# A state space's injection operator made in the layout of its use, from powers laid out through memory, in a hybrid convolution and S5 layer on one Trainium2 core

## The chip, the core and the metric

The kernel runs on one core of a Trainium2 chip. Its engines take their instructions in order, each from its own queue: TensorE (PE) for matmuls and transposes, VectorE (DVE) and ScalarE (ACT) for elementwise work, GpSimd (POOL), and SyncE (SP), which here issues all DMAs. The metric is the device time of one execution in microseconds (us), as a median over runs. The weights' and inputs' layout in the chip's memory is made on the host before, which isn't timed.

## What is computed

One layer over 1024 positions of 1024 channels. In short, with all else of the reference cut:

```python
h = rms_norm(x, pre_g)
conv_in, z_c, u_s, z_s, g_c, g_s = split(h @ w_in)
ca, cb = split(conv_in, 2)
cu = causal_depthwise_conv(ca * sigmoid(cb))            # 31 taps
conv_out = (silu(layer_norm(cu)) * silu(z_c)) @ w_conv_out
# S5: 32 groups of 16 channels, each drives 64 complex states
bbar = z * b                # z (zr, zi) from lambda and the step, per state
s[t] = a * s[t-1] + bbar @ u[t];   y[t] = Re(c @ s[t]) + d * u[t]
y = gelu(y);  y = y * sigmoid(y @ w_glu + b_glu)
ssm_out = (y * silu(z_s)) @ w_ssm_out
out = (sigmoid(g_c) * conv_out + sigmoid(g_s) * ssm_out) @ w_out
result = x + rms_norm(out, post_g)
```

The S5 part is computed in 128 blocks of 8 positions. Within a group, the injection operator R takes the 8 x 16 inputs (position j in the block, channel h) of a block to its 128 state numbers (64 real, 64 imaginary): an entry is a power of a, which depends on j and the state, times an entry of bbar, which depends on the state and h. A scan over the 128 blocks then gives the states.

## The kernel before

**Products.** Every projection is a product of 1024 positions with 128 output channels, a *unit*, named by its weight: cb and ca (convolution), gc, gs (gates), zc, zs, glu, so, co. To keep float32's precision the weights and the activations are split in two parts: the high parts wh (ACT, `wsplit_h`) and the remainder wl = wr - wh (DVE, `wsplit_l`, L718) of the raw weight wr. Each step k over 128 input channels makes three passes (wh with xh, wh with xl, wl with xh) of two matmuls of 128x512 (`product`, L735, matmuls at L743). A unit has eight steps, a glu or so unit four. Within the unit before, wh is made at the third step and wl at the fifth, and then SP is given the next raw weight's load (`wload`, L700). Two buffers each are there for wr, wh and wl.

**The order.** Units follow a list: cb0 ca0 gc0 cb1 ca1 gc1 to gc7 cb2 ca2 zc0 zc1 cb3 ca3 zc2 zc3, then the glu units, which need the S5's result y, and the rest. Between the k steps other work is put in by a planner that runs while the program is recorded: `Clock` (L640 to L676) holds tasks written as generators, each `yield cost, delay` says how long VectorE is taken and how long the task then rests, and `tick(1.296)` after each k step runs what is due by this model's time. So the order on each engine is fixed in the program, and moves when a task's steps or delays change. The chip keeps each engine's order and waits on semaphores.

**The state space.** The tasks are `s5_params` (L206 to L366, parameters from lambda and the step) and `s5_chain` (L788), which runs `s5_quarter(c)` (L370) for four quarters c of 8 groups. Numbers behind names, as in RT0, are quarters. A quarter does in order:

- DVE: RT = PR * bbar and tmp = sPI * bsw (L397, L399, by `mul`, L387) and their sum (L401): the injection operator with the states on the partitions, 128x1024; PR, PI and sPI are powers, bsw is bbar with its parts swapped.
- PE: eight transposes rp (L404); ACT: the copy R (L406). Now (j, h) lies on the partitions.
- PE: ep = R times U (L416), the inputs of each block taken to the states. U comes through memory (us_scratch, L200).
- DVE: the output operator O (L387, L417); PE: kp (L437, L438), the 8 x 8 blocks within a block, spread into Mt by eight DMAs (L458).
- DVE: an angle ta, tb, tk, rounded and corrected (L446 to L461); ACT: its sines (L463 to L465); DVE: Et, the scan Zs (L476); a swap of halves Zw by two DMAs (L479); then Zw times the sine and Sx (L490).
- PE: yp (L496, L497); ACT: gelu yt (L501); SP: to ys_scratch and back as y32 in another layout (eight DMAs, L507).

After all quarters y is split into yh and yl (L797, L798) for the glu units. DVE also has the convolution's 31 taps (pp and acc, L545), whose input is ext (L517 to L521), and whose starting values ACT makes (L536 to L538).

128x1024 tiles of all these tasks come from one pool of 21 buffers (`T`). PSUM has two buffers "aux" for the state space and two "mm" for the products.

Of the kernel before, what the change touches and what calls it, by code (L numbers as in the profile page):

```python
# [35 lines left out]
def tile_hybrid_block(  # L36
# [16 lines left out]
    bmat: bass.AP,  # L53
    cmat: bass.AP,
    dmat: bass.AP,
    ident_in: bass.AP,
    cst_in: bass.AP,
    iota_in: bass.AP,
# [2 lines left out]
    nc = tc.nc  # L61
    V, A, G, PE = nc.vector, nc.scalar, nc.gpsimd, nc.tensor
# [10 lines left out]
    zc_scr = nc.dram_tensor("zc_scratch", (8, 128, 1024), F32, kind="Internal").ap()  # L73
    us_scr = nc.dram_tensor("us_scratch", (4, 128, 1024), F32, kind="Internal").ap()
    ys_scr = nc.dram_tensor("ys_scratch", (4, 128, 1024), F32, kind="Internal").ap()
    gc_scr = nc.dram_tensor("gc_scratch", (8, 128, 1024), F32, kind="Internal").ap()

    def T(name, dt=F32):
        return tp.tile([128, 1024], dt, tag="T", name=name)

    def PS(name, tag):
        return ps.tile([128, 1024], F32, tag=tag, name=name)
# [4 lines left out]
    ident = const.tile([128, 128], F32, name="ident")  # L87
    cst = const.tile([128, 4], F32, name="cst")
# [8 lines left out]
    iota = const.tile([128, 128], F32, name="iota")  # L97
# [108 lines left out]
    def s5_params(P):  # L206
# [12 lines left out]
        def tt(o, a, b, op):  # L219
            V.tensor_tensor(out=o, in0=a, in1=b, op=op)  # L220
            return o
# [26 lines left out]
        f = st("turnf")  # L248
        s = st("turns")
# [12 lines left out]
        q3 = nt()  # L262
# [31 lines left out]
        PR = const.tile([128, 9, 32], F32, name="PR")  # L294
        PI = const.tile([128, 9, 32], F32, name="PI")
        sPI = const.tile([128, 9, 32], F32, name="sPI")
# [45 lines left out]
        zr = tt(nt(), n1, n2, ALU.add)  # L342
        zr = tt(st("zr"), zr, rden, ALU.mult)
# [4 lines left out]
        sz = st("sz")  # L348
# [4 lines left out]
        bbar, bsw = bb[:, 0], bb[:, 1]  # L353
        tmp = T("bbtmp")
# [8 lines left out]
        tt(tmp, bmt[:, 0], szb, ALU.mult)  # L363
        yield 1.8, 0
        tt(bsw, bsw, tmp, ALU.subtract)
        P.update(PR=PR, PI=PI, sPI=sPI, nPR=nPR, r8=r8, bbar=bbar, bsw=bsw, tauh=tauh, taul=taul)  # L366

    y32 = {}

    def s5_quarter(c, P):  # L370
        g0 = c * 8
# [2 lines left out]
        def v4(t):  # L374
            return t.rearrange("p (g j h) -> p g j h", g=8, j=8)
# [4 lines left out]
        def pw(t, lo):  # L380
            return t[:, lo:lo + 8, gs].rearrange("p j g -> p g j").unsqueeze(3).to_broadcast([128, 8, 8, 16])

        def bc(t):
            return t[:, gs, :].unsqueeze(2).to_broadcast([128, 8, 8, 16])

        def mul(o, x0, x1):
            V.tensor_tensor(out=o, in0=x0, in1=x1, op=ALU.mult)  # L387

        def pe(f, cost):
            for g in range(8):  # L390
                f(g, slice(g * 128, (g + 1) * 128))
            clk.now += cost


        RT = T(f"RT{c}")
        tmp = T(f"tmp{c}")
        mul(v4(RT), pw(P["PR"], 0), bc(P["bbar"]))  # L397
        yield 1.15, 0
        mul(v4(tmp), pw(P["sPI"], 0), bc(P["bsw"]))  # L399
        yield 1.15, 0  # L400
        V.tensor_tensor(out=RT, in0=RT, in1=tmp, op=ALU.add)  # L401
        yield 1.15, 2.5
        rp = PS(f"rp{c}", "aux")
        pe(lambda g, s: PE.transpose(rp[:, s], RT[:, s], ident), 0.9)  # L404
        R = T(f"R{c}")
        A.activation(out=R, in_=rp, func=AF.Copy)  # L406
        U = usU[c]

        O1 = T(f"O1_{c}")
# [71 lines left out]
        if c < 3:  # L481
# [7 lines left out]
        V.memset(v3(Sx)[:, :, 0:1], 0.0)  # L489
        V.tensor_tensor(out=v3(Sx)[:, :, 1:128], in0=v3(Et)[:, :, 0:127], in1=v3(Zw)[:, :, 0:127],  # L490
                        op=ALU.subtract)
        yield 1.2, 4.5
        yp = PS(f"yp{c}", "aux")

# [183 lines left out]
    clk = Clock()  # L678
# [108 lines left out]

    def s5_chain():  # L788
        yield from s5_params(P5)
        for c in range(4):  # L790
            while not P5_ready[0]:
                yield 0.0, 0.5
            yield from s5_quarter(c, P5)
        yield 0.0, 5.0
        for c in range(4):
            yh[c], yl[c] = T(f"yh{c}", F32R), T(f"yl{c}", F32R)
            A.activation(out=yh[c], in_=y32[c], func=AF.Copy)  # L797
            V.tensor_tensor(out=yl[c], in0=y32[c], in1=f32(yh[c]), op=ALU.subtract)  # L798
            yield 1.15, 0
        s5_done[0] = True  # L800
        yield 0.0, 0.0
# [301 lines left out]
    for j in range(2):  # L1103
# [9 lines left out]
WARM = 3  # L1113

_INS = ["x", "xt", "w_us", "w_in", "w_co", "w_glu", "w_so", "w_out", "pre_g", "post_g", "conv_w", "chan",
        "bglu", "lam", "bmat", "cmat", "dmat", "ident", "cst", "iota"]


def _layout(inp):
    import numpy as np  # L1120

    f = np.float32
    d = {}
    d["x"] = inp["x"][0]
    d["xt"] = inp["x"][0].reshape(128, 8, 1024).transpose(2, 1, 0).reshape(8, 128, 1024)
    w = inp["w_in"][0]
    d["w_us"] = w[:, 3072:3456].reshape(4, 2, 128, 384).transpose(0, 2, 1, 3).reshape(4, 128, 768)

    def stat(a):
        k, m = a.shape  # L1130
        return a.reshape(k // 128, 128, m // 128, 128).transpose(2, 1, 0, 3).reshape(m // 128, 128, k)

    wi = stat(w)
    d["w_in"] = wi
    d["w_co"] = stat(inp["w_conv_out"][0])
    d["w_glu"] = stat(inp["w_ssm_glu"][0])
    d["w_so"] = stat(inp["w_ssm_out"][0])
    d["w_out"] = inp["w_out"][0].reshape(8, 128, 1024)
    d["pre_g"] = inp["pre_norm_gain"][0].reshape(8, 128).T
    d["post_g"] = inp["post_norm_gain"][0]  # L1140
    cw = np.concatenate([inp["conv_w"][0][::-1], np.zeros((1, 1024), f)], 0)
    d["conv_w"] = cw.reshape(32, 8, 128).transpose(2, 1, 0)
    col = lambda a: a.reshape(-1, 128).T
    d["chan"] = np.stack([col(inp["conv_b"][0]), col(inp["conv_ln_gain"][0]), col(inp["conv_ln_bias"][0])], 1)
    d["bglu"] = col(inp["b_ssm_glu"][0])
    lr, li = inp["ssm_lambda_re"][0].T, inp["ssm_lambda_im"][0].T
    ldt = np.broadcast_to(inp["ssm_log_dt"][0][None, :], (64, 32))
    d["lam"] = np.stack([np.concatenate([a, a], 0) for a in (ldt, lr, li)], 1)
# [35 lines left out]
```

## Time and profile before

| | |
|---|---|
| median of 3 runs | 827.98 us (827.82 to 828.73) |
| the profiled execution | 828.06 us |
| its span | 826.2 us |
| PE busy | 813.8 us |
| DVE busy | 622.7 us |
| ACT busy | 277.6 us |
| mean granted TensorE clock | 0.997 |

The span runs from the first to the last instruction that the profile shows; 1.86 us of the execution lie around it. Busy time is that of an engine's own instructions; an engine that waits, or only issues DMAs, isn't busy. In a timeline row stand the start, the duration, the engine, the line, the operation with output and input, and in brackets an idle time ahead of it and what ended it. Matmuls overlap, so the time that one takes from the engine is read from start to start.

### The profile page before, as it was taken

The page shows a single profiled execution, that of the slowest core. Times are in us where ns is not written, and L with a number is a line of the kernel's source. Part 1 is how long each engine was busy: PE and PEld are TensorE (multiplying, and loading weights), DVE is VectorE, ACT ScalarE, POOL GpSimd, SP SyncE. Part 2 cuts the span into 40 slices and gives each one's busy share as a digit, 9 for nine tenths or more (in the row PEclk, how much of TensorE's full clock was granted, in tenths as well). Part 3 has the DMA queues.
Part 4 walks back from the last instruction along what each step waited for, and adds up shares of the span by engine and source line. Part 5 has one row for each costly group of instructions (what it writes and reads, how often), then busy time and mean ns, then how long its engine had stood idle before and what let it go on. Part 6 is the DMA issues. An engine that isn't in the chain of part 4 may idle for free.

```text
span 826.2 us, 9707 instructions
## 1 busy us (share of the span) xinstructions
PE 813.8 (98%) x3806; PEld 672.6 (81%) x3806; DVE 622.7 (75%) x902; ACT 277.6 (34%) x300; POOL 25.6 (3%) x27
## 2 busy tenths in 40 slices
PE   9999999999999999999999999999999999999996
PEld 6878888888878887888888888888887888888885
DVE  4699897798998989998999889398496644442242
ACT  5862623535315344323321031222257211131121
POOL 3400000000000000000000000000000000000010
PEclk9999999999999999999999999999999999999998
DMA  9703544463534312111112112122262644425142
GB/s 345 282 35 120 168 102 128 100 195 91 137 109 110 106 52 90 51 52 52 39 38 102 52 52 103 51 90 90 102 199 82 229 153 153 153 76 178 61 171 99
DMA packets 40364, 94.97 MB, mean 115 GB/s; under 512 B 8880, under 2 KB 17712, under 8 KB 40320
## 3 DMA queue, kind: packets, MB, share of 16 engines
q1 hardware_dynamic: 40320, 94.36, 34.2%
q8 instruction: 30, 0.49, 0.2%
q14 instruction: 14, 0.11, 0.0%
HBM read 68.00 MB, written 20.97 MB: 108 GB/s over the span
## 4 chain that ended last, share of the span: by engine, by line
PE 76%; DVE 14%; ACT 3%; DMA 3%; issue 2%; POOL 1%; SPq 1%; DVEq 0%; POOLq 0%; ACTq 0%
PE pgs L743 11%; PE pco L743 11%; PE po L1037 10%; PE pcb L743 9%; PE pca L743 8%; PE pzc L743 7%; PE pzs L743 5%; PE pgc L743 5%; PE pso L743 5%; DVE pp L545 3%; PE pgl L743 2%; DVE acc L545 2%; DMA Zw<-Zs 1%; DVE xt L173 1%; PE ep L416 1%
## 5 line engine op out<-in xcount | busy, mean ns | idle before, releaser
L545 DVE SCALAR_TENSOR_TENSOR pp<-ext,cw,pp 128x512 f32<-128x512 f32 x232 | 165.2, 744 | 5.4 <-ACT pp L536 5.4
L545 DVE SCALAR_TENSOR_TENSOR acc<-ext,hs,acc 128x512 f32<-128x512 f32 x120 | 89.3, 744 | 0.0
L1037 PE MATMUL po<-wox,mgh 128*128 128x512 f32 x192 | 52.3, 389 | 0.0
L521 ACT ACTIVATE ext<-ext 128x1179 f32<-128x1179 f32 x8 | 9.5, 1192 | 101.4 <-DVE ext L520 101.4
L1037 PEld LDWEIGHTS po<-wox,mgh 128*128 128x128 f32 x192 | 36.0, 188 | 7.5
L743 PE MATMUL pcb<-xh,wl_cb 128*128 128x512 f32 x128 | 39.6, 391 | 0.9 <-DVE wl_cb L718 0.9
L743 PE MATMUL pgc<-xh,wh_gc 128*128 128x512 f32 x128 | 40.4, 397 | 0.0
L1009 DVE TENSOR_TENSOR sgr<-pco,sgr 128x1024 f32<-128x1024 f32 x8 | 9.8, 1224 | 40.2 <-PE pco L743 40.2
L743 PE MATMUL pca<-xh,wh_ca 128*128 128x512 f32 x128 | 40.0, 393 | 0.0
L743 PE MATMUL pzc<-xh,wh_zc 128*128 128x512 f32 x128 | 39.8, 392 | 0.0
L743 PE MATMUL pgs<-xh,wh_gs 128*128 128x512 f32 x128 | 39.7, 392 | 0.0
L743 PE MATMUL pca<-xh,wl_ca 128*128 128x512 f32 x128 | 39.5, 390 | 0.1
L743 PE MATMUL pcb<-xh,wh_cb 128*128 128x512 f32 x128 | 39.5, 390 | 0.0
L743 PE MATMUL pgc<-xh,wl_gc 128*128 128x512 f32 x128 | 39.5, 390 | 0.0
L743 PE MATMUL pco<-cuh,wl_co 128*128 128x512 f32 x128 | 39.5, 390 | 0.0
L743 PE MATMUL pgc<-xl,wh_gc 128*128 128x512 f32 x128 | 39.5, 389 | 0.0
L743 PE MATMUL pzc<-xl,wh_zc 128*128 128x512 f32 x128 | 39.5, 389 | 0.0
L743 PE MATMUL pgs<-xl,wh_gs 128*128 128x512 f32 x128 | 39.5, 389 | 0.0
L743 PE MATMUL pco<-cuh,wh_co 128*128 128x512 f32 x128 | 39.4, 389 | 0.0
L743 PE MATMUL pca<-xl,wh_ca 128*128 128x512 f32 x128 | 39.4, 389 | 0.0
L743 PE MATMUL pcb<-xl,wh_cb 128*128 128x512 f32 x128 | 39.4, 389 | 0.0
L743 PE MATMUL pco<-cul,wh_co 128*128 128x512 f32 x128 | 39.4, 389 | 0.0
(273 smaller groups left out, 1760.2 us busy)
## 6 DMA issues: line engine op xcount, KB each, us to landing
xt<-in_xt_dram SPq DMA_DIRECT2D x8, 512.0 KB, 6.2
xin<-in_x_dram SPq DMA_DIRECT2D x8, 512.0 KB, 9.8
wr_cb<-in_w_in_dram SPq DMA_DIRECT2D x8, 512.0 KB, 3.4
wr_ca<-in_w_in_dram SPq DMA_DIRECT2D x8, 512.0 KB, 3.2
wr_gc<-in_w_in_dram SPq DMA_DIRECT2D x8, 512.0 KB, 3.9
gc_scratch<-gct SPq DMA_DIRECT2D x8, 512.0 KB, 3.6
wr_zc<-in_w_in_dram SPq DMA_DIRECT2D x8, 512.0 KB, 3.2
zc_scratch<-zct SPq DMA_DIRECT2D x8, 512.0 KB, 2.6
```

The source lines that it names most:

```text
L173: V.scalar_tensor_tensor(out=xraw[k], in0=xraw[k], scalar=gcol[:, k:k + 1], in1=rbc, op0=ALU.mult, op1=ALU.mult)
L416: pe(lambda g, s: PE.matmul(epp[:, s], lhsT=R[:, s], rhs=U[:, s], start=True, stop=True), 1.8)
L521: A.activation(out=ext[:, :, 0:3, 1:132], in_=ext[:, :, 4:7, 0:131], func=AF.Copy)
L545: V.scalar_tensor_tensor(out=o, in0=src(e, r), scalar=w, in1=o, op0=ALU.mult, op1=ALU.add)
L743: PE.matmul(p[:, js(j)], lhsT=lhs[:, ks], rhs=rhs(k, j), start=st, stop=sp_)
L1009: V.tensor_tensor(out=sgt, in0=p, in1=sgt, op=ALU.mult)
L1037: PE.matmul(p[:, js(j)], lhsT=lhs[k][:, s], rhs=rhs[k][:, js(j)], start=st, stop=sp_)
```

## The change

The injection operator is no longer made with the states on the partitions and transposed. Its entries are regrouped: power times z, which depends on j and the state alone, and the raw input matrix b, which is an input of the kernel. Both are brought into the layout with (j, h) on the partitions by DMAs.

- `s5_params` has six more DVE operations of 128x256, which make the powers times z, real and swapped (qpw).
- `inj_powers`: four transposes of them (qp) on PE, one copy qt of 128x512 on ACT, two DMAs that write qs_scratch in memory.
- `inj_in(c)`, for each quarter: two loads of 512 KB of a new input bt, which the host has laid out and repeated (in..c, in..d), and sixteen loads of 64 KB, each of which reads one row of 4 KB of qs_scratch into sixteen partitions (eight each for in..a and in..b). For quarter 0 it stands in `s5_chain` ahead of the quarters with a rest of 7 model us behind it, for the others ahead of the yield at Sx of the quarter before.
- `s5_quarter`: in..a times in..c, in..b times in..d, and their sum, in place and in the same sizes as the three operations of before. The transposes rp and the copy R are gone.

```diff
@@ s5_params
+        qpw = T("qpw")
+        q3 = [qpw[:, i * 256:(i + 1) * 256].rearrange("p (j g) -> p j g", j=8) for i in range(3)]
+        zrj = zr.unsqueeze(1).to_broadcast([128, 8, 32])
+        szj = sz.unsqueeze(1).to_broadcast([128, 8, 32])
+        yield 0.6, 0
+        tt(q3[0], PR[:, 0:8, :], zrj, ALU.mult)
+        tt(q3[2], sPI[:, 0:8, :], szj, ALU.mult)
+        tt(q3[0], q3[0], q3[2], ALU.subtract)
+        yield 1.0, 0
+        tt(q3[1], PR[:, 0:8, :], szj, ALU.mult)
+        tt(q3[2], sPI[:, 0:8, :], zrj, ALU.mult)
+        tt(q3[1], q3[1], q3[2], ALU.add)
+        P["qpw"] = qpw
+        yield 1.0, 0
...
+    def inj_powers(P):
+        qpw = P.pop("qpw")
+        qp = PS("qp", "aux")
+        for b in range(2):
+            for a in range(2):
+                i = (b * 2 + a) * 128
+                PE.transpose(qp[:, i:i + 128], qpw[:, a * 256 + b * 128:a * 256 + b * 128 + 128], ident)
+        clk.now += 0.45
+        qt = T("qt")
+        A.activation(out=qt[:, 0:512], in_=qp[:, 0:512], func=AF.Copy)
+        for b in range(2):
+            nc.sync.dma_start(out=qs_scr[:, 4 * b:4 * b + 4].rearrange("a j g s -> (j g) a s"),
+                              in_=qt[:, b * 256:(b + 1) * 256].rearrange("p (a s) -> p a s", a=2))
+
+    def inj_in(c):
+        inj[c] = [T(f"in{c}{n}") for n in "abcd"]
+        for r in range(2):
+            nc.sync.dma_start(out=inj[c][2 + r], in_=bt[c, r])
+        for r in range(2):
+            for j in range(8):
+                src = qs_scr[r, j, c * 8:c * 8 + 8].rearrange("g s -> (g s)")
+                nc.sync.dma_start(out=inj[c][r][16 * j:16 * j + 16], in_=src.partition_broadcast(16))
...
@@ s5_quarter
-        RT = T(f"RT{c}")
-        tmp = T(f"tmp{c}")
-        mul(v4(RT), pw(P["PR"], 0), bc(P["bbar"]))
+        R, Rb, B0, B1 = inj.pop(c)
+        mul(R, R, B0)
         yield 1.15, 0
-        mul(v4(tmp), pw(P["sPI"], 0), bc(P["bsw"]))
+        mul(Rb, Rb, B1)
         yield 1.15, 0
-        V.tensor_tensor(out=RT, in0=RT, in1=tmp, op=ALU.add)
-        yield 1.15, 2.5
-        rp = PS(f"rp{c}", "aux")
-        pe(lambda g, s: PE.transpose(rp[:, s], RT[:, s], ident), 0.9)
-        R = T(f"R{c}")
-        A.activation(out=R, in_=rp, func=AF.Copy)
+        V.tensor_tensor(out=R, in0=R, in1=Rb, op=ALU.add)
+        del Rb, B0, B1
+        yield 1.15, 0
...
+        if c < 3:
+            inj_in(c + 1)
         yield 1.2, 4.5
...
@@ s5_chain
         yield from s5_params(P5)
+        while not P5_ready[0]:
+            yield 0.0, 0.5
+        inj_powers(P5)
+        yield 0.0, 0.0
+        inj_in(0)
+        yield 0.0, 7.0
         for c in range(4):
-            while not P5_ready[0]:
-                yield 0.0, 0.5
             yield from s5_quarter(c, P5)
```

The planner's order moves with it. On DVE, in the first quarter, from the last parameter operations on (usT are the four blocks of the input u, scaled; wl_cb1 is the remainder of the weights of unit cb1). Before:

```order
L387 TENSOR_TENSOR RT0_713<-PR_402,bb_677 128x1024
L387 TENSOR_TENSOR tmp0_714<-sPI_404,bb_677 128x1024
L401 TENSOR_TENSOR RT0_713<-RT0_713,tmp0_714 128x1024
L192 TENSOR_TENSOR usT1_463<-usT1_463,rbc_433 128x1024
L516 MEMSET ext0_739 128x2x4x4
L517 TENSOR_TENSOR ext0_739<-pca0_622,sg0_641 128x2x4x128
L520 TENSOR_TENSOR ext0_739<-ext0_739 128x528
L387 TENSOR_TENSOR O1_0_769<-nPR_405,cmt_124 128x1024
L387 TENSOR_TENSOR otmp0_771<-PI_403,cmt_124 128x1024
L718 TENSOR_TENSOR wl_cb1_779<-wr_cb1_590,wh_cb1_750 128x1024
```

After, at the same place:

```order
L222 TENSOR_TENSOR qpw_713<-qpw_713 128x256
L194 TENSOR_TENSOR usT1_463<-usT1_463,rbc_433 128x1024
L556 MEMSET ext0_772 128x2x4x4
L557 TENSOR_TENSOR ext0_772<-pca0_622,sg0_641 128x2x4x128
L560 TENSOR_TENSOR ext0_772<-ext0_772 128x528
L194 TENSOR_TENSOR usT2_465<-usT2_465,rbc_433 128x1024
L758 TENSOR_TENSOR wl_cb1_799<-wr_cb1_590,wh_cb1_783 128x1024
L429 TENSOR_TENSOR in0a_742<-in0a_742,in0c_744 128x1024
L429 TENSOR_TENSOR in0b_743<-in0b_743,in0d_745 128x1024
L442 TENSOR_TENSOR in0a_742<-in0a_742,in0b_743 128x1024
L429 TENSOR_TENSOR O1_0_831<-nPR_405,cmt_124 128x1024
```

The products of the injection operator have moved behind usT2 and wl_cb1, and the output operator behind them; on PE, ep of this quarter moves from the eighth step of gc0 to the fifth of cb1, and kp from cb1's third step to its eighth.

On DVE, from the scan of the first quarter to its Sx (wl_gc1 and wl_gc2 are remainders of weights, Et, Zs, Zw tiles of the quarter, pp and acc taps). Before:

```order
L387 TENSOR_TENSOR Et0_809<-Zs0_957,tb0_863 128x1024
L718 TENSOR_TENSOR wl_gc1_991<-wr_gc1_781,wh_gc1_955 128x1024
L545 SCALAR_TENSOR_TENSOR pp0_832<-ext0_739,cw_82,pp0_832 128x512
L545 SCALAR_TENSOR_TENSOR acc0_831<-ext0_739,hs_83,acc0_831 128x4x128
L545 SCALAR_TENSOR_TENSOR pp0_832<-ext0_739,cw_82,pp0_832 128x512
L387 TENSOR_TENSOR Zw0_966<-Zw0_966,tk0_865 128x1024
L489 MEMSET Sx0_1024 128x8
L490 TENSOR_TENSOR Sx0_1024<-Et0_809,Zw0_966 128x8x127
```

After:

```order
L429 TENSOR_TENSOR Et0_872<-Zs0_1018,tb0_925 128x1024
L556 MEMSET ext1_1053 128x2x4x4
L557 TENSOR_TENSOR ext1_1053<-pca1_950,sg1_967 128x2x4x128
L560 TENSOR_TENSOR ext1_1053<-ext1_1053 128x528
L429 TENSOR_TENSOR Zw0_1027<-Zw0_1027,tk0_927 128x1024
L758 TENSOR_TENSOR wl_gc2_1079<-wr_gc2_887,wh_gc2_1064 128x1024
L527 MEMSET Sx0_1089 128x8
L528 TENSOR_TENSOR Sx0_1089<-Et0_872,Zw0_1027 128x8x127
```

The remainder that follows the Et product now follows the product on Zw, and it is that of gc2; wl_gc1 has moved ahead of the scan.

On ACT, around the gelu of the last quarter (yt3), ahead of the glu units (pp2 and acc2 are starting values of the third convolution block, yh the high parts of y). Before:

```order
L710 ACTIVATE wh_zc2_2232<-wr_zc2_2103 128x1024
L501 ACT_TABLE_LOAD
L501 ACTIVATE yt3_2251<-yp3_2234 128x1024
L536 ACTIVATE pp2_2261<-ext2_1938,cw_82 128x512
L537 ACTIVATE pp2_2261<-ext2_1938,nb1_84,cw_82 128x512
L538 ACTIVATE acc2_2260<-ext2_1938,hs_83 128x4x128
L797 ACTIVATE yh0_2324<-y32_0_1092 128x1024
L797 ACTIVATE yh1_2335<-y32_1_1475 128x1024
L521 ACTIVATE ext3_2345<-ext3_2345 128x3x3x131
L710 ACTIVATE wh_zc3_2356<-wr_zc3_2181 128x1024
L797 ACTIVATE yh2_2358<-y32_2_1879 128x1024
L797 ACTIVATE yh3_2368<-y32_3_2281 128x1024
```

After:

```order
L750 ACTIVATE wh_zc2_2273<-wr_zc2_2110 128x1024
L561 ACTIVATE ext3_2339<-ext3_2339 128x3x3x131
L750 ACTIVATE wh_zc3_2350<-wr_zc3_2215 128x1024
L541 ACT_TABLE_LOAD
L541 ACTIVATE yt3_2391<-yp3_2374 128x1024
L576 ACTIVATE pp2_2404<-ext2_1964,cw_82 128x512
L577 ACTIVATE pp2_2404<-ext2_1964,nb1_84,cw_82 128x512
L578 ACTIVATE acc2_2403<-ext2_1964,hs_83 128x4x128
L841 ACTIVATE yh0_2421<-y32_0_1190 128x1024
L841 ACTIVATE yh1_2431<-y32_1_1596 128x1024
L841 ACTIVATE yh2_2442<-y32_2_1997 128x1024
```

yt3 and what follows it now stand behind ext3 and wh_zc3: on PE, yp of the last quarter has moved from the third step of ca3 to the sixth of zc2, while the glu units stay where they were.

More of the change, by code (lines that the diff above doesn't have):

```diff
@@ L55, in tile_hybrid_block @@
     dmat: bass.AP,
+    bt: bass.AP,
     ident_in: bass.AP,
@@ L75, in tile_hybrid_block @@
     ys_scr = nc.dram_tensor("ys_scratch", (4, 128, 1024), F32, kind="Internal").ap()
+    qs_scr = nc.dram_tensor("qs_scratch", (2, 8, 32, 128), F32, kind="Internal").ap()
     gc_scr = nc.dram_tensor("gc_scratch", (8, 128, 1024), F32, kind="Internal").ap()
@@ L365, in s5_params @@
         tt(bsw, bsw, tmp, ALU.subtract)
+        qpw = T("qpw")
[12 more added lines that the diff above has]
+        yield 1.0, 0
         P.update(PR=PR, PI=PI, sPI=sPI, nPR=nPR, r8=r8, bbar=bbar, bsw=bsw, tauh=tauh, taul=taul)
     y32 = {}
+    inj = {}
+    def inj_powers(P):
[19 more added lines that the diff above has]
+                nc.sync.dma_start(out=inj[c][r][16 * j:16 * j + 16], in_=src.partition_broadcast(16))
     def s5_quarter(c, P):
@@ L1115 @@
 _INS = ["x", "xt", "w_us", "w_in", "w_co", "w_glu", "w_so", "w_out", "pre_g", "post_g", "conv_w", "chan",
-        "bglu", "lam", "bmat", "cmat", "dmat", "ident", "cst", "iota"]
+        "bglu", "lam", "bmat", "cmat", "dmat", "bt", "ident", "cst", "iota"]
 def _layout(inp):
@@ L1150, in _layout @@
     d["bmat"] = np.stack([np.concatenate([br, bi], 0), np.concatenate([bi, br], 0)], 1)
+    bt = d["bmat"].reshape(128, 2, 4, 8, 16).transpose(2, 1, 4, 3, 0)
+    d["bt"] = np.broadcast_to(bt[:, :, None], (4, 2, 8, 16, 8, 128)).reshape(4, 2, 128, 1024)
     cr, ci = inp["ssm_c_re"][0].transpose(2, 0, 1), inp["ssm_c_im"][0].transpose(2, 0, 1)
```

## The prediction

> **What bounds the kernel now.** I read the page's busy shares first, then TensorE's waits, then the timelines of PE, DVE, ACT and SP around the first quarter of the state space, and last the stretch where its result is first used.
>
> ```profile
> span 826.2 us, 9707 instructions
> PE 813.8 (98%) x3806; PEld 672.6 (81%) x3806; DVE 622.7 (75%) x902; ACT 277.6 (34%) x300; POOL 25.6 (3%) x27
> ```
>
> TensorE is busy in 813.8 of 826.2 us. So microseconds can leave only as PE work or as PE waits, and each new PE wait costs its full length. These are its waits:
>
> ```profile
> PE ep L416 <- ACT R L406: 1.3, 1, 1.3
> PE pgl L743 <- DVE wl_glu L718: 0.5, 1, 0.5
> PE yp L497 <- DVE Sx L490: 0.4, 1, 0.4
> ```
>
> Two of them belong to the state space: ep waits once for the copied R, and yp once for Sx. What the removed transposes cost PE is read in its timeline (start, duration, engine, line):
>
> ```profile
> 73.76 0.61 PE L743 MATMUL pgc<-xh,wh_gc 128*128 128x512 f32 x2
> ...
> 78.75 0.62 PE L743 MATMUL pgc<-xh,wl_gc 128*128 128x512 f32 x2
> 79.20 1.03 PE L404 MATMUL rp<-ident,RT 128*128 128x128 f32 x8
> 80.00 0.71 PE L743 MATMUL pgc<-xh,wh_gc 128*128 128x512 f32 x2
> 80.54 0.62 PE L743 MATMUL pgc<-xl,wh_gc 128*128 128x512 f32 x2
> ...
> 84.17 1.95 PE L416 MATMUL ep<-U,R 128*128 128x128 f32 x16
> 85.88 0.71 PE L743 MATMUL pgc<-xh,wh_gc 128*128 128x512 f32 x2
> ...
> 90.14 0.21 PE L437 MATMUL kp<-O,bb 128*16 128x16 f32 x2
> ...
> 92.18 0.50 PE L743 MATMUL pcb<-xh,wh_cb 128*128 128x512 f32 x1
> ```
>
> The matmul pairs start every 0.453 us (78.75 to 79.20). A group of eight transposes takes 0.80 (79.20 to 80.00), and the pair behind it 0.54 instead of 0.45: 0.89 a quarter. A k step of a product is three pairs, 1.36 us, and a unit of eight steps 10.88. The ep group takes 1.71 + 0.09 (84.17 to 85.88), kp 2.04 (90.14 to 92.18).
>
> **PE work and the two waits.** Four quarters lose 4 x 0.89 = 3.55 us. The new qp group has four transposes: 4 x 0.10 + 0.09 = 0.49. Net -3.06. Nothing transposes R any more, so its wait goes: -1.30. What is late next at that place is the in-place sum of in3a and in3b. Their loads stand in SP's queue directly behind the wr_cb3 load, which goes out as Sx of the quarter before is made; ep3 comes only in the second zc unit, more than two units later, so nothing. The wait of yp for Sx of the second quarter goes too, since yp1 moves from gc5 to gc6: -0.36. Together -4.72, the gain that is there to be lost again.
>
> The three full-width DVE operations per quarter stay three of the same size. ACT loses four copies of 1.02 and is 34% busy, so that is worth nothing.
>
> **qpw and qp.** In before, DVE goes from the last parameter operation straight to the R products:
>
> ```profile
> 72.60 0.68 DVE L220 TENSOR_TENSOR bb<-bb,bbtmp 128x512 f32<-128x512 f32 x1
> 73.20 1.22 DVE L387 TENSOR_TENSOR RT<-PR,bb 128x1024 f32<-128x1024 f32 x1
> ...
> 89.85 1.23 DVE L446 TENSOR_TENSOR tk<-ta,tb 128x1024 f32<-128x1024 f32 x1
> 93.29 0.28 DVE L451 TENSOR_TENSOR kr<-kp,dmt 16x128 f32<-16x128 f32 x1 [2.21 <-ACT kr L450]
> 93.50 0.67 DVE L454 TENSOR_SCALAR tk<-tk 128x1024 f32<-128x1024 f32 x1
> ...
> 97.74 0.75 DVE L545 SCALAR_TENSOR_TENSOR pp<-ext,cw,pp 128x512 f32<-128x512 f32 x1
> ```
>
> No row has 128x256; halfway between none and 128x512 (0.68, pitch 0.60 from 72.60 to 73.20) I take 0.34 to 0.45 each, the larger where one needs the one before. The six then end at 73.20 + 2.3 = 75.5. PE comes to qp after one k step of gc0, at 73.76 + 1.36 = 75.12, and waits: +0.5 with the hand-over (0 to 0.9).
>
> **When R of the first quarter is ready.** qp ends near 76.0; the copy qt of 128x512 takes 0.7 (the row of pp below) and waits for nothing else, so the write to qs_scratch goes out near 77.0. Then sixteen loads of 64 KB stand one behind the other on SP, the first waiting until the write has landed. Two rows say how fast SP issues such loads, and three how long they take to land:
>
> ```profile
> 63.40 3.65 SPq L200 DMA_DIRECT2D U<-us_scratch  x8
> 93.63 5.72 SPq L458 DMA_DIRECT2D Mt<-kr  x8
> U<-us_scratch SPq DMA_DIRECT2D x32, 64.0 KB, 3.3
> ys_scratch<-yt SPq DMA_DIRECT2D x4, 512.0 KB, 2.6
> y<-ys_scratch SPq DMA_DIRECT2D x32, 64.0 KB, 2.4
> Mt<-kr SPq DMA_DIRECT2D x4, 24.0 KB, 2.0
> ```
>
> U's issue is 0.456 each, Mt's 0.72. The loads of in0a have U's form, a row of memory into sixteen partitions, and y's size and source, so I take 0.456 and 2.4. The write lands like ys_scratch, 2.6: first load issued at 79.6, last at 79.6 + 15 x 0.456 = 86.4, in0b whole at **88.8**. The other ends: 0.33 and 2.0 give 86.6, 0.72 and 3.3 give 93.7. The Trainium skill ("DMA: Bandwidth & Descriptors", Anatomy of one DMA — SWDGE (gpsimd) path) fits 2.0 us and 436 KB per us, an estimate of 2.15 for 64 KB; by it all that hangs on this load would come 0.25 earlier, and the y row, measured here on SP, stands above it.
>
> DVE has nothing to do meanwhile but usT, ext and wl_cb1, done by 82.0: in order, it stands before in0a and then in0b for more than 5 us. R is there at 88.8 + 1.25 + 1.23 = 91.3. PE reaches ep0, now in cb1 after four steps, at 73.76 + 0.49 + 0.5 + 10.88 + 5.44 = 91.07: +0.2.
>
> **The weight splits behind it.** From in0b to the corrected angle stand on DVE eleven full-width operations and wl_ca1 (1.14 each, 1.25 where one needs the one before; the Et and yl rows below show both), two taps (0.66 apart) and three short ones of 1.1 together: 16.65. Then ACT makes the sines, a table load, sg and wh_gc1, as in before from 96.72 to 103.45:
>
> ```profile
> 96.72 1.16 ACT L463 ACTIVATE tk<-ta,cst 128x1024 f32<-128x1024 f32 x1 [1.22 <-DVE ta L461]
> 102.40 1.05 ACT L710 ACTIVATE wh_gc<-wr_gc 128x1024 fp32r<-128x1024 f32 x1
> ```
>
> 6.75, and wl_gc1 another 1.2: ready at 88.8 + 24.6 = 113.4. PE needs it 0.9 us into gc1: after ep0 come 1.8 for ep, four steps 5.44, kp 2.04, ca1 10.88 and 0.9, so 91.27 + 21.06 = 112.3. Wait **+1.1**.
>
> wl_gc2 has changed sides: in before it stood ahead of the product on Zw, now behind it. The Zw swap goes through memory:
>
> ```profile
> 100.86 1.22 DVE L387 TENSOR_TENSOR Et<-Et,tb 128x1024 f32<-128x1024 f32 x1
> 102.12 1.23 DVE L471 TENSOR_TENSOR Et<-Et,E 128x1024 f32<-128x1024 f32 x1
> 103.38 2.63 DVE L476 TENSOR_TENSOR_SCAN Zs<-r,Et 128x128 f32<-128x128 f32 x8
> 106.05 1.23 DVE L387 TENSOR_TENSOR Et<-Zs,tb 128x1024 f32<-128x1024 f32 x1
> ...
> 111.17 1.23 DVE L387 TENSOR_TENSOR Zw<-Zw,tk 128x1024 f32<-128x1024 f32 x1 [0.78 <-DMA Zw<-Zs]
> ```
>
> From scan's end, 106.0, to 111.17 are 5.2. After wl_gc1 come 2.5 of Et, 2.65 of scan, 5.2, 1.15 of Zw and 1.2 of wl_gc2: 12.7. PE asks again after 10.88: **+1.8** (0 if PE is ahead of wl_gc1). The same pair in quarter 1 (wl_gc6) has 1 to 2 us to spare, those of the later quarters more.
>
> **The glu.** yp3 moves from the third step of ca3 to the sixth of zc2. Behind it wait yt, the starting values of pp2, five pairs of taps and yh, yl of all four quarters; in before all that was done well before wl_glu:
>
> ```profile
> 278.58 1.03 ACT L501 ACTIVATE yt<-yp 128x1024 f32<-128x1024 f32 x1 [4.38 <-PE yp L497]
> 279.50 0.72 ACT L536 ACTIVATE pp<-ext,cw 128x512 f32<-128x512 f32 x1
> 280.12 0.81 ACT L537 ACTIVATE pp<-ext,nb,cw 128x512 f32<-128x512 f32 x1
> 279.63 0.33 SPq L502 DMA_DIRECT2D ys_scratch<-yt  x1
> 282.25 3.65 SPq L507 DMA_DIRECT2D y<-ys_scratch  x8
> 286.81 2.35 DVE L798 TENSOR_TENSOR yl<-y,yh 128x1024 fp32r<-128x1024 f32 x2
> 314.12 0.68 DVE L718 TENSOR_TENSOR wl_glu<-wr_glu,wh_glu 128x512 fp32r<-128x512 f32 x1
> ```
>
> From yp3's end on: pp2 ready at 2.4; seven taps to 7.05; yl0 to yl2 to 10.5; yl3 to 11.65 (y32_3 lands at 1.05 + 2.6 + 3.2 + 2.4 = 9.3, yh3 follows); four taps and wl_glu0 to 14.9; eleven taps to 22.2; wl_glu1 to 22.8. PE needs wl_glu0 at 2.72 + 10.88 + 0.9 = 14.5 and wl_glu1 5.44 after its start: waits 0.4 and 2.4. The 0.49 of before is part of them: **+2.3** (0 to 3). This is a backlog and not a loss: later DVE waits for PE, so it costs once.
>
> **Sum.** 828.06 (the profiled execution: span 826.2 and 1.86 around it; 0.08 above the median) - 4.72 + 0.5 + 0.2 + 1.1 + 1.8 + 2.3 = 829.24; against the median **829.2**. About 0.2%, 1.66 us, is what a measurement of this kernel can tell from no change: 826.3 to 829.6.
>
> One rule speaks against the change as a whole. Measured, 128x128 transposes cost 0.10 us each on a PE that hardly waits for them. The Trainium skill ("VectorE: DVE Perf Modes", The three transpose paths) also sends a 128x128 transpose to TensorE where PSUM will do as its destination. The trace agrees with it; the sum has it already as the small -3.06.
>
> **Rivals.** *The waits stay hidden (faster).* If in0b is whole by 85.7, wl_gc1 and wl_gc2 (88.8 + 37.3 at the earliest, against 123.0) are both in time, the 3.1 fall away: 826.1. Without the glu backlog alone, 826.9; without both, 823.8. For it: DVE has 25% idle, and issue at 0.33 comes within a microsecond of this. Against: the sixteen loads are in series behind a write that has to land. Chance 0.26.
>
> *The loads are slow (slower).* If sixteen small loads are issued like Mt's, 0.72 each, in0b is whole at 79.6 + 10.8 + 2.4 = 92.8. R, every wl behind it and PE follow one for one: 829.2 + 4.0 = 833.2; with 3.3 to land at U's pitch, 830.1. It decides from 89.2 on, where the sum passes 829.6. For it: 1 MB of input bt is loaded beside them and U needed 3.3. Against: Mt's loads go from tile to tile and are of many sizes, another form. The Trainium skill ("DMA: Bandwidth & Descriptors", Rules for kernel authors) calls transfers under 64 KB mostly overhead and says to coalesce; the 2.0 for 24 KB beside 2.4 for 64 KB agrees. Chance 0.34.
>
> **How the numbers follow.** The forecast has 0.40, own range 827.0 to 830.5. The 80% range takes in 826.1 with part of the glu term gone and 833.2, and leaves out both waits gone together and 0.72 with 3.3: 825.5 to 833.2. Faster than 826.3: 0.24, nearly all of the first rival. Slower than 829.6: 0.36, the second rival and a little of the forecast, which lies near that edge. The rest, 0.40.
>
> **What would show it.** Right: a DVE idle of 5 us before in0a and in0b near 82, R's sum ending near 91, PE waits for wl_gc1 and wl_gc2 of 1 to 2 us each, two for wl_glu with 2 to 3 us together, none for R or Sx, PE busy 3 us less. Wrong: in0b whole before 86 or after 90, a PE wait at ep1, ep2 or ep3, or wl_glu in time.

## The result, and where the time went

The changed kernel took 839.91 us (median of 4 runs, 838.44 to 841.37) against 827.9: a ratio of 1.014, with a 95% interval of 1.0128 to 1.0153. It is 12 us slower, nearly 7 us above the top of the predicted range. Its profiled execution took 841.37, the longest of the four, with a span of 839.5; its rows are compared with the span of before, 826.2, and the sums below are those of this execution.

The waits of TensorE (PE) in the changed kernel; in before they were 5.3 us together, 1.6 of them the warm-up, which stayed:

```profile
PE pgl L783 <- DVE wl_glu L758: 3.8, 2, 2.2
PE pgc L783 <- DVE wl_gc L758: 3.1, 1, 3.1
PE pgc L783 <- DVE Sx L527: 2.4, 2, 1.4
PE ep L454 <- DVE in0a L442: 1.8, 1, 1.8
PE pgs L783 <- DVE wl_gs L758: 1.4, 1, 1.4
```

With six small ones they make 14.8 without the warm-up, against 3.7 before. The two put down to Sx are at the first use of wl_gc2 and of wl_gc6: the remainder is made just ahead of Sx. The second largest wait ends at 199.01, at wl_gc7, and what follows it runs slower. First PE there, then windows of 1 us around it (the third number from the right is the granted clock):

```profile
195.30 0.61 PE L783 MATMUL pgc<-xl,wh_gc 128*128 128x512 f32 x2
199.01 1.22 PE L783 MATMUL pgc<-xh,wl_gc 128*128 128x512 f32 x2 [3.10 <-DVE wl_gc L758]
200.03 1.05 PE L783 MATMUL pgc<-xh,wh_gc 128*128 128x512 f32 x2
200.88 1.05 PE L783 MATMUL pgc<-xl,wh_gc 128*128 128x512 f32 x2
```

```profile
198.00:199.00 1.00, 0.00 (x0) 0.00 (x0) 1.00 (x2) 0.00 (x0) 0.00 (x0) 0.77 0.30 115
199.00:200.00 1.00, 0.99 (x2) 0.83 (x3) 1.00 (x1) 0.00 (x0) 0.91 (x1) 0.50 0.11 29
200.00:201.00 1.00, 1.00 (x4) 0.78 (x3) 1.00 (x2) 0.00 (x0) 0.05 (x1) 0.50 0.37 108
202.00:203.00 1.00, 1.00 (x9) 0.91 (x9) 1.00 (x3) 0.00 (x0) 0.00 (x0) 1.00 0.55 161
```

Pairs start every 0.85 us instead of 0.45: the clock is at half for 3.4 us, to 202.0, which costs 1.5. The same happens behind the second wait for wl_glu, from 324.8 to 328.2, for 1.7. The Trainium skill ("TensorE: Matmul & The Clock Gate", Why this matters for your kernels) says to leave TensorE no idle gap over about 3 us; the gap of 3.10 agrees, the one of 2.16 ahead of 324.3 was enough too.

The sum: removed PE work -3.06 (the prediction's figure), waits 14.8 - 3.7 = +11.1, half clock +3.2, together +11.2 of the 13.3 between the two spans. Of the rest, 0.6 stands ahead of the change. Much of the other 1.5 is, by an estimate, that a wait costs more than its idle time: the one of 1.35 for wl_gc6 puts off the next pair by 1.51 and the one behind by 0.12 more (starts at 179.18, 181.14 and 181.71), and there are seven waits more than in before.

Why VectorE (DVE) is late: the loads. SP's issue and the median time to landing, of the first and the third quarter:

```profile
79.42 4.78 SPq L410 DMA_DIRECT2D in0a<-qs_scratch  x8
85.11 3.90 SPq L410 DMA_DIRECT2D in0b<-qs_scratch  x8
182.46 8.27 SPq L410 DMA_DIRECT2D in2a<-qs_scratch  x8
190.78 3.96 SPq L410 DMA_DIRECT2D in2b<-qs_scratch  x8
```

```profile
in0a<-qs_scratch SPq DMA_DIRECT2D x8, 64.0 KB, 5.1
in0b<-qs_scratch SPq DMA_DIRECT2D x8, 64.0 KB, 2.3
in2d<-in_bt_dram SPq DMA_DIRECT2D x1, 512.0 KB, 8.4
in2a<-qs_scratch SPq DMA_DIRECT2D x8, 64.0 KB, 7.0
in2b<-qs_scratch SPq DMA_DIRECT2D x8, 64.0 KB, 2.3
```

The eight loads right behind the 1 MB of bt land in 5 to 7 us, the eight behind those in 2.3. While the first are out, SP can't issue the others at its pace. Each DMA here waits for the eighth before it: the last load of in2a goes out at 190.43, as in2d, issued at 182.00, lands. SP's own wait there:

```profile
SPq L410 <- DMA in2d<-in_bt_dram: 3.8, 1, 3.8
```

In the first quarter SP waits 1.3 for in0d and 0.9 for the first of in0a. On DVE, in order, a weight remainder stands behind them (timeline, in brackets the idle time):

```profile
87.13 1.23 DVE L429 TENSOR_TENSOR in0a<-in0a,in0c 128x1024 f32<-128x1024 f32 x1 [4.53 <-DMA in0b<-qs_scratch]
90.97 1.23 DVE L429 TENSOR_TENSOR in0b<-in0b,in0d 128x1024 f32<-128x1024 f32 x1 [2.62 <-DMA in0b<-qs_scratch]
...
192.68 1.23 DVE L429 TENSOR_TENSOR in2a<-in2a,in2c 128x1024 f32<-128x1024 f32 x1 [3.03 <-DMA in2a<-qs_scratch]
196.59 1.23 DVE L429 TENSOR_TENSOR in2b<-in2b,in2d 128x1024 f32<-128x1024 f32 x1 [2.69 <-DMA in2b<-qs_scratch]
197.74 1.22 DVE L758 TENSOR_TENSOR wl_gc<-wr_gc,wh_gc 128x1024 fp32r<-128x1024 f32 x1
```

wl_gc7 has had its inputs since 190.8, when wh_gc7 was done; it is made at 197.74 because in2a and in2b stand ahead of it. In the glu the late thing is yp3, which ends at 300.23, 13.5 us ahead of the first glu unit (313.68). ScalarE (ACT) makes the starting values pp of the third convolution block behind yt3, and DVE's taps wait for them:

```profile
300.27 1.03 ACT L541 ACTIVATE yt<-yp 128x1024 f32<-128x1024 f32 x1 [0.37 <-PE yp L537]
301.19 0.71 ACT L576 ACTIVATE pp<-ext,cw 128x512 f32<-128x512 f32 x1
```

```profile
301.94 1.46 DVE L585 SCALAR_TENSOR_TENSOR pp<-ext,cw,pp 128x512 f32<-128x512 f32 x2 [2.08 <-ACT pp L576]
...
311.86 1.23 DVE L842 TENSOR_TENSOR yl<-y,yh 128x1024 fp32r<-128x1024 f32 x1 [1.75 <-ACT yh L841]
...
315.65 0.68 DVE L758 TENSOR_TENSOR wl_glu<-wr_glu,wh_glu 128x512 fp32r<-128x512 f32 x1
...
323.55 0.68 DVE L758 TENSOR_TENSOR wl_glu<-wr_glu,wh_glu 128x512 fp32r<-128x512 f32 x1
```

### The profile page after: what moved, and what is told of

Its sections match the earlier page's. It is cut to its first block, busy times and chain, and to the rows that moved or that the text cites. A ratio compares the mean times of both kernels' runs of the same rounds, so it can differ in the third digit from the quotient of the medians.

```text
span 839.5 us, 9787 instructions
## 1 busy us (share of the span) xinstructions
PE 816.1 (97%) x3778; PEld 671.8 (80%) x3778; DVE 624.7 (74%) x908; ACT 274.7 (33%) x297; POOL 26.3 (3%) x27
## 4 chain that ended last, share of the span: by engine, by line
PE 64%; DVE 16%; DMA 8%; SPq 4%; issue 3%; ACT 3%; POOL 1%; DVEq 0%; POOLq 0%; ACTq 0%
PE pco L783 10%; PE pgs L783 10%; PE po L1081 10%; PE pzc L783 7%; PE pca L783 6%; PE pcb L783 6%; PE pzs L783 5%; PE pso L783 4%; PE pgl L783 2%; DVE pp L585 2%; SPq L410 1%; DVE xt L175 1%; SPq L496 1%; DMA in2d<-in_bt_dram 1%; DVE wl_gc L758 1%
## 5 line engine op out<-in xcount | busy, mean ns | idle before, releaser
L783 PE MATMUL pgs<-xh,wl_gs 128*128 128x512 f32 x128 | 39.5, 390 | 1.4 <-DVE wl_gs L758 1.4
L783 PE MATMUL pzc<-xh,wl_zc 128*128 128x512 f32 x128 | 39.5, 390 | 0.6 <-DVE wl_zc L758 0.6
```

Source lines behind the costliest of these rows:

```text
L783: PE.matmul(p[:, js(j)], lhsT=lhs[:, ks], rhs=rhs(k, j), start=st, stop=sp_)
```

## The experiments

Theories at the start: A, the loads arrive late (A1 because of the bytes of bt ahead of them, B because of the number of small loads), DVE stands before them with weight remainders behind, PE follows; C, the planner's new order alone makes the time; D, the glu wait is a term of its own. The runs of the kernel before beside them had medians of 828.15 to 828.42.

**No loads.**

```diff
-        for r in range(2):
-            nc.sync.dma_start(out=inj[c][2 + r], in_=bt[c, r])
...
-                nc.sync.dma_start(out=inj[c][r][16 * j:16 * j + 16], in_=src.partition_broadcast(16))
+        for t in inj[c]:
+            nc.gpsimd.memset(t, 0.01)
```

> Leaves out all loads of the quarters' operands: GpSimd fills the four tiles of each quarter with a constant where the 18 loads stood, so R is not the reference's; the order on DVE, ACT and TensorE stays that of after. Theory A (the loads arrive late, DVE stands before them in its order and the weight remainders behind it make TensorE wait): the waits at ep0 (1.8), wl_gc2 (1.1), gc6 (1.4) and gc7 (3.1, with some 1.7 for the halved clock behind it) go, some 8 to 9 us; the glu waits stay: about 831. Theory C (the new order alone, with wl behind Zw and the glu right behind yp3, makes the time): 838 to 840.

832.0 (ratio 1.0046, 1.0031 to 1.0061): 8 us of the loss go, as A had it, and with them every idle time of DVE at in..a and in..b. What stays:

```profile
PE pgl L779 <- DVE wl_glu L754: 3.3, 2, 2.1
PE pgs L779 <- DVE wl_gs L754: 1.4, 1, 1.4
PE pgc L779 <- DVE Sx L523: 1.1, 1, 1.1
```

So there are two causes: the loads, and something in the order.

**The input matrix loaded once.** `inj_in` loads bt for c = 0 only, and all quarters use those two tiles.

```diff
+        if c == 0:
+            inj["b"] = [T("in0c"), T("in0d")]
+            for r in range(2):
+                nc.sync.dma_start(out=inj["b"][r], in_=bt[c, r])
...
-        R, Rb, B0, B1 = inj.pop(c)
+        R, Rb = inj.pop(c)
+        B0, B1 = inj["b"]
```

> Loads the input matrix tiles only for quarter 0 and uses them in all quarters (so quarters 1 to 3 use the wrong input matrix); the sixteen loads of powers stay in every quarter. Theory A1 (the 1 MB of bt issued just ahead keeps the small loads from landing): in1a, in2a and in3a land in 2 to 3 us instead of 6 to 7, DVE no longer stands at in2a and in2b for 5.7 us, the wait for wl_gc7 and the halved clock behind it go: 839.9 - 5 = about 835, first quarter and glu unchanged. Theory B (the number of small loads, issued by SP in turn, is what takes the time): landing and time as after, 839 to 841. Theory C: as after.

835.34 (1.0079, 1.0062 to 1.0096), as A1 has it: the wait for wl_gc7 is gone. The small loads land sooner, though not at 2 to 3 us:

```profile
in1a<-qs_scratch SPq DMA_DIRECT2D x8, 64.0 KB, 3.8
in2a<-qs_scratch SPq DMA_DIRECT2D x8, 64.0 KB, 4.8
in3a<-qs_scratch SPq DMA_DIRECT2D x8, 64.0 KB, 3.7
```

Some of the delay stays; the loads of U and of weights stand ahead of them too, and were not tried apart.

**One load per tile of powers.**

```diff
-            for j in range(8):
-                src = qs_scr[r, j, c * 8:c * 8 + 8].rearrange("g s -> (g s)")
-                nc.sync.dma_start(out=inj[c][r][16 * j:16 * j + 16], in_=src.partition_broadcast(16))
+            src = qs_scr[r, :, c * 8:c * 8 + 8].rearrange("j g s -> j (g s)")
+            nc.sync.dma_start(out=inj[c][r], in_=src.unsqueeze(1).to_broadcast([8, 16, 1024]))
```

> Each of the two tiles of powers is one load of 512 KB instead of eight of 64 KB; all else as after. Theory B (many small loads): the operands of a quarter are whole some 8 us after the first bt load instead of 12 to 14, so ep0 and gc7 hardly wait: 832 to 835. Theory A1 (bytes ahead in the DMA engines): the same 2 MB has to go through and takes 6 to 9 us behind U and the weights, a part of that gain: 835 to 838. Theory C: as after.

845.5 (1.0217, 1.0191 to 1.0243): slower than after by 5.6 us, which none of the theories had. The powers come later, not sooner (DVE in the first quarter, then SP):

```profile
89.58 1.23 DVE L428 TENSOR_TENSOR in0a<-in0a,in0c 128x1024 f32<-128x1024 f32 x1 [7.52 <-DMA in0a<-qs_scratch]
92.51 1.23 DVE L428 TENSOR_TENSOR in0b<-in0b,in0d 128x1024 f32<-128x1024 f32 x1 [1.70 <-DMA in0b<-qs_scratch]
```

```profile
79.26 0.76 SPq L409 DMA_DIRECT2D in0a<-qs_scratch  x1
80.06 0.59 SPq L409 DMA_DIRECT2D in0b<-qs_scratch  x1
80.75 0.87 SPq L196 DMA_DIRECT2D us_scratch<-usT  x2
82.09 0.34 SPq L739 DMA_DIRECT2D wr_gc<-in_w_in_dram  x1
```

SP is through at 80.7 instead of 89.0, and issues 1.5 MB of others at once, which in after go out behind the powers. That these share the DMA engines with them fits the rows, but wasn't tried by itself. The windows show something else too (the last two numbers are the mean busy share of the 16 DMA engines and GB/s):

```profile
81.00:82.00 1.00, 1.00 (x7) 0.81 (x6) 1.00 (x1) 0.00 (x0) 0.00 (x0) 1.00 1.04 397
91.00:92.00 1.00, 0.21 (x1) 0.00 (x0) 0.00 (x0) 0.00 (x0) 0.00 (x0) 1.00 0.51 205
```

From 89 to 95 the share stays at 0.48 to 0.52, and at 0.50 to 0.51 from 141 to 146 in the second quarter; eight or nine packets are under way there at a time, against sixteen at 85.5. So the powers come over half of the engines at half the rate: as an estimate, 1 MB takes 5.1 us at 205 GB/s and 2.6 at 397. The load's pattern has eight rows outermost; whether that is the reason, no run tried. So this run changes the rate of the loads with their number and is no clean test of B. What speaks against B is the run before, which kept the number and gained. The Trainium skill ("DMA: Bandwidth & Descriptors", Rules for kernel authors) says to coalesce many small transfers; here, with the same bytes, the coalesced form cost 5.6 us more, but on half of the engines, so the run doesn't decide on that rule.

**The glu one unit later.** The unit zc4 is moved ahead of the glu units.

```diff
-    seq += [("yhl", 0)] + glu + zs[0:1] + pairs[4] + zs[1:4] +
+    seq += zc[4:5] + [("yhl", 0)] + glu + zs[0:1] + pairs[4] + zs[1:4] +
...
-    pairs[7] + zc[4:6] + gso[4]
+    pairs[7] + zc[5:6] + gso[4]
```

> After, with the unit zc4 moved ahead of the glu units, so that one more unit of 10.9 us lies between yp3 and the glu. Theory D (the glu term: VectorE's backlog behind yp3 makes TensorE wait 3.8 us for wl_glu and then run at half clock for 3 us): both go, 839.9 - 5 = about 835. Rival: the backlog isn't absorbed and comes back as a wait for another weight remainder: 839 to 841.

842.05 (1.0166, 1.0151 to 1.0181): the rival. The wait for wl_glu goes, and one for wl_zc, 2.7, comes in the same place: the backlog meets whatever remainder is next. D as a thing of the glu units alone falls: zc4 now starts as soon behind yp3, 13.5 us, as the glu units did, and its remainder is no earlier. The 2 us over after needn't be the edit's: ahead of it, in this execution, PE waits 2.8 at ep0 instead of 1.8, with half the clock behind it, and 3.9 for wl_gc7 instead of 3.1.

**No loads, and no rest.** As the first, and the rest ahead of the quarters is taken out.

```diff
-        yield 0.0, 7.0
+        yield 0.0, 0.0
```

> As e1 (the operands are filled in by GpSimd, so R is not the reference's; no loads of them), and the rest of 7 model us ahead of the quarters is taken out, so that the planner puts the quarters nearly where they stood in before (yp of the last quarter at the eighth step of ca3 instead of the sixth of zc2; in before the third). Theory C' (what e1 still loses, 832.0 against 828, comes from the later place of the quarters, by the glu wait and what follows it): the glu waits shrink to under 1.5 us and the removed transposes show: 824 to 827. Otherwise it stays at 831 to 833.

822.05 (0.9928, 0.9915 to 0.994): 10 us below the first experiment by that constant alone, and 6 us faster than before. yp3 now ends 21.6 us ahead of the first glu unit, and 0.7 of the glu waits is left, though the starting values still stand behind yt3. This is what the change is worth when its operands cost nothing and the order suits.

**The kernel before, moved.**

```diff
         for c in range(4):
-            while not P5_ready[0]:
-                yield 0.0, 0.5
+        while not P5_ready[0]:
+            yield 0.0, 0.5
+        yield 0.0, 8.5
+        for c in range(4):
```

> The kernel before, all its operations, with a rest of 8.5 model us ahead of the quarters: rp0 moves from gc0 to cb1, yp of the last quarter from ca3 to the fourth step of zc2. Theory C' : TensorE waits for wl_glu twice, 3 to 4 us, and runs at half clock behind it, with further waits behind the backlog: 828 + 4 to 7 = 832 to 835. If the place of the quarters costs nothing: 827 to 829.

828.19 (1.0002, 0.9992 to 1.0011): no change, so this place costs nothing. It has no wait for wl_glu at all, though its last yp stands only two steps ahead of where after has it. In its order ACT makes the third block's starting values ahead of yt3, and DVE has no taps waiting for them between yp3 and yl. That gave theory E: what costs is work that PE needs soon, put behind a late thing in an engine's order.

For the glu, the rows of ACT, DVE and PE speak for something simpler:

```profile
291.39 1.03 ACT L501 ACTIVATE yt<-yp 128x1024 f32<-128x1024 f32 x1
305.09 0.69 DVE L718 TENSOR_TENSOR wl_glu<-wr_glu,wh_glu 128x512 fp32r<-128x512 f32 x1
306.71 0.62 PE L743 MATMUL pgl<-yh,wh_glu 128*128 128x512 f32 x2
```

yp3 ends at 290.54 here. The first wl_glu is done 15.2 us later, against 16.1 in after, so the order of the starting values changes it by 0.9 at most. The first glu unit starts 16.2 us behind yp3, against 13.5 in after, and PE asks for the remainder 0.9 into it, at 17.1 against 14.4. So after waits some 1.7 (1.64 measured) and this kernel doesn't. The two steps of the place are worth more than the order, and that a yp3 as late as after's costs nothing isn't shown.

**Loads of quarters 1 to 3 a quarter earlier.** `inj_in(c + 1)` is moved from Sx to right behind the sum R.

```diff
         del Rb, B0, B1
         yield 1.15, 0
+        if c < 3:
+            inj_in(c + 1)
...
-        if c < 3:
-            inj_in(c + 1)
         yield 1.2, 4.5
```

> After, with the operands of quarters 1 to 3 loaded right behind the sum R of the quarter before, some 30 us earlier than after does it; the order on VectorE, ScalarE and TensorE is that of after, all loads and results as after. Theory A: VectorE no longer stands at in1, in2 and in3, the waits for wl_gc7 (3.1, and the half clock behind it) and wl_zc go, the first quarter and the glu stay: 833 to 836. If the loads' bytes cost by themselves wherever they are: 838 to 841.

832.73 (1.0058, 1.0044 to 1.0071): 7 us less than after, with all loads. By the medians, against the first experiment's 832.0, the first quarter's loads would be worth under 1 us and those of quarters 1 to 3 nearly all of the 8. The clock blurs that: the glu waits are those of after, 3.8, but the half clock behind them, 1.7, is missing here, while the profile of the first experiment has it. PE waits 1.5 at ep0 here and not at all there. So, by the profiles, the first quarter's loads cost about 1.5, and the others between 5 and 6 of the 7.

**The first quarter earlier too.** As that; the six operations of qpw stand ahead of those of bbar, bsw is out, the rest is 5.0.

```diff
-        tt(bsw, bmt[:, 1], zrb, ALU.mult)
-        tt(tmp, bmt[:, 0], szb, ALU.mult)
-        tt(bsw, bsw, tmp, ALU.subtract)
...
-        yield 0.0, 7.0
+        yield 0.0, 5.0
```

> Full computation. As e8, and for the first quarter: the powers qpw are made ahead of bbar, so qp stands at the sixth step of ca0; three operations of 128x512 that made bsw, which nothing reads any more, are out; the rest ahead of the quarters is 5 model us, so that the quarters stand where before has them (yp of the last at the second step of ca3). Theories A and C' together: no wait at ep, wl_gc or wl_glu of over 1 us: 823 to 826, faster than before by 0.3 to 0.6%. If the loads' bytes slow the weights' and U's loads: 827 to 831.

841.49 (1.0159, 1.0145 to 1.0173): a miss. TensorE waits 7.7 us for wh_cb1, which ACT makes behind ext0, which DVE makes behind in0a and in0b: the rest was too short for loads that landed at 88. Theory E's pattern over two engines.

**The same with the rest at 11**, and bt of the first quarter loaded ahead of qpw and bbar.

```diff
+        inj_bt(0)
         yield 1.5, 0
         bb = T("bb").rearrange("p (r g h) -> p r g h", r=2, g=32)
...
-        yield 0.0, 5.0
+        yield 0.0, 11.0
```

> Full computation. As e9, but the input matrix of the first quarter is loaded ahead of the parameters' last part, and the rest ahead of the quarters is 11 model us: in0a then stands behind ext0 and wl_cb1 on VectorE (in e9 ahead of both), and the starting values of the third convolution block stand ahead of yt of the last quarter on ScalarE (in after behind it). Theory E (what costs is work that stands behind a late thing in an engine's order: wl behind in..a, taps and wl_glu behind starting values behind yt): no wait over 1.5 us: 823 to 826. If the loads' bytes themselves cost: 830 or more.

824.76 (0.9959, 0.9947 to 0.9971): faster than before, and no wait of PE behind the first cb unit is over 1.1 us.

**Early loads with the rest at 12.** Quarters 1 to 3 as with the early loads above, the first as in after but for the rest.

```diff
-        yield 0.0, 7.0
+        yield 0.0, 12.0
```

> Full computation. As e8 (operands of quarters 1 to 3 loaded a quarter earlier), and the rest ahead of the quarters 12 model us instead of 7: ep0 moves to the second step of ca1, some 5 us behind the landing of in0b, and the starting values of the third convolution block move ahead of yt of the last quarter. Theory E: the waits at ep0 and at wl_glu go: 823 to 826. If the place of the quarters costs as such: 832 to 835.

824.39 (0.9962, 0.9947 to 0.9977): the waits at ep0 and for wl_glu are gone, as E has it.

**Early loads with a rest of 0.**

```diff
-        yield 0.0, 7.0
+        yield 0.0, 0.0
```

> Full computation. As e8 with a rest of 0: the order of e6 (822 without loads), now with the loads. VectorE comes to in0a some 4 us sooner and stands before it until 91 with ep0 due at 87: theory E: TensorE waits 5 to 7 us at ep0, with a halved clock behind it (1.7), and little elsewhere: 828 to 831. If late operands of the first quarter are absorbed: 823 to 825.

840.46 (1.0147, 1.0134 to 1.016). The order that gave 822 without loads loses 18 us with them. The wait falls in the first quarter, as expected, but elsewhere and longer: PE waits 10.0 us for wh_cb1, not 5 to 7 at ep0, later 3.2 for Sx, and the clock is at half for 10.2 and 3.4 us with these.

**After with one constant changed.** The loads stay where after has them.

```diff
-        yield 0.0, 7.0
+        yield 0.0, 12.0
```

> Full computation; after with one constant changed, the rest ahead of the quarters 12 model us instead of 7. The loads of quarters 1 to 3 stay at Sx of the quarter before. Theory E: the first quarter and the glu no longer wait (that is worth about 5 to 7 us), VectorE still stands at in1, in2 and in3 for some us: 829 to 835. If the late loads alone made after slow: 838 to 841.

823.55 (0.9943, 0.9931 to 0.9956): faster than before by 4.7 us, than after by 16, and better than every theory had it, E too. PE's waits, without the small ones:

```profile
PE pcb L783 <- DVE wl_cb L758: 1.2, 1, 1.2
PE kp L475 <- DVE O L457: 1.2, 2, 0.9
```

The loads of the first and third quarter are as late as in after: in0b starts at 91.72, against 90.97, and DVE's idle time before in2b is the same 2.69. What has moved is the remainder of gc7:

```profile
182.24 1.22 DVE L758 TENSOR_TENSOR wl_gc<-wr_gc,wh_gc 128x1024 fp32r<-128x1024 f32 x1
...
190.60 1.23 DVE L429 TENSOR_TENSOR in2a<-in2a,in2c 128x1024 f32<-128x1024 f32 x1 [1.18 <-DMA in2a<-qs_scratch]
194.52 1.23 DVE L429 TENSOR_TENSOR in2b<-in2b,in2d 128x1024 f32<-128x1024 f32 x1 [2.69 <-DMA in2b<-qs_scratch]
```

It stands ahead of in2a, not behind in2b. So late loads cost little where no remainder stands behind them: what is left is the 1.2 for O, which stands behind in2b and in3b. That is theory E, for the loads. For the glu it is the place again, in ACT, DVE and PE:

```profile
283.37 1.03 ACT L541 ACTIVATE yt<-yp 128x1024 f32<-128x1024 f32 x1 [11.53 <-PE yp L537]
300.32 0.68 DVE L758 TENSOR_TENSOR wl_glu<-wr_glu,wh_glu 128x512 fp32r<-128x512 f32 x1
303.58 0.61 PE L783 MATMUL pgl<-yh,wh_glu 128*128 128x512 f32 x2
```

yp3 ends at 283.33, 20.2 us ahead of the glu units instead of 13.5, and in the two other kernels under 825 it is 20.2 too. wl_glu is done 17.7 behind yp3, later than after's 16.1, although the starting values stand ahead of yt3. No run moved the starting values alone.

The three kernels with full computation under 825 have intervals that overlap; what the early loads add to the right rest isn't resolved.

## Why the prediction was wrong, point by point

- **PE work and the two waits, -4.72.** Right in kind: the transposes and both waits are gone, and in the three kernels under 825, which have no half clock between the first unit and the last, PE is busy 809.4 to 810.8 us against 813.8. That the one with only the rest changed gains the same 4.7 as a whole is luck, since it has waits of its own.
- **qp, +0.5.** 0.2.
- **In0b whole at 88.8.** 90.97. The first load went out at 79.42, as forecast, and those of in0b landed in 2.3, close to "2.4 to land". What failed is the pitch of 0.456 for all sixteen: the last went out at 88.52 instead of 86.4, since SP waited 1.3 for in0d and 0.9 for the first of in0a. For in0a "2.4 to land" failed too, with 5.1: the loads of y go out once their own write has landed, with nothing else close ahead of them, and in0a goes out behind 1 MB of bt. The bytes of bt stood in the prediction only as a point for a rival. R was 2 us late and PE waited 1.8 at ep0 instead of 0.2.
- **wl_gc1 +1.1, wl_gc2 +1.8.** The order of DVE was read rightly, the sizes not. wl_gc1 was done 2.2 us later than forecast, but PE came to it 3.0 later, behind ep0, and the wait was gone; for wl_gc2 1.1 was measured.
- **"The same pair in quarter 1 (wl_gc6) has 1 to 2 us to spare, those of the later quarters more."** The step that cost most. It was said of the Zw pair; wl_gc6 waited 1.4. That wl_gc7 stands behind in2a and in2b was not looked for, and for the late loads the prediction asked only when ep needs them: "ep3 comes only in the second zc unit, more than two units later, so nothing." The question for a moved load is not when its own result is needed but what stands behind its reader: 3.1 us there, and the clock, 1.5.
- **The glu, +2.3.** The mechanism was right, with waits of 1.6 and 2.2 for 0.4 and 2.4: PE came at 14.4 behind yp3 (14.5 forecast), and wl_glu was done at 16.1 (14.9 forecast). The half clock behind it added 1.7.
- **The half clock** is in no term: 3.2 us in the profiled execution. Nor is the wait of 1.4 for wl_gs, which ends at 506.10; it is there without the loads too, and in none of the three kernels under 825.
- **The slow rival** had the right kind of mechanism (late loads, R, remainders, PE), but in the first quarter alone and with the wrong price: it put the lateness in SP's pitch of 0.72 and gave 833.2. SP was held up by loads that hadn't landed, bt's among them, and most of the loss lies in the quarters behind.

## What to carry to other kernels

Where engines run in a fixed order, cost a moved or added load by what stands behind its reader in that engine's order, and what stands behind that on the next engine. Price the landing by a row with the same traffic ahead of it, not by the same size alone. For work that waits for a late result, set the time until the next operand is needed against the backlog in between. And when a planner sets the order from modelled times, vary its delays before judging a change: one constant was 16 us here, about three times what the change itself is worth.

## What the runs showed of the hardware

- Gaps of 2.1 to 3.9 us in TensorE's work were mostly followed by 3.4 us at half the granted clock, which costs another 1.5 to 1.7; gaps of up to 1.8 never were. With gaps of 7.7 and 10.0 the clock stood at half for 6.8 and 10.2 us. It isn't the length alone: a gap of 2.2 ahead of ep0 (input matrix loaded once) and one of 2.3 for wl_zc (one load per tile) left the clock alone, and so did the two glu waits of the kernel with early loads and the rest of 7, 3.8 together like those of after (310 to 330):

```profile
310.00:330.00 20.00, 17.84 (x79) 14.47 (x78) 20.00 (x29) 6.74 (x7) 0.00 (x0) 1.00 0.30 103
```

- One 512 KB load that spreads eight rows of 4 KB over sixteen partitions each wasn't faster than eight of 64 KB: with it half of the DMA engines were busy (share 0.51, 205 GB/s), and with the usual 512 KB loads all (1.04, 397).
